# An instance norm on one core: 28 of 32 units joined in pairs, with rows of 64 KB

## The chip, the core and the metric

The kernel runs on one core of a Trainium2 chip. Its time is the device time of one execution in microseconds (us); the time before is the median of three runs. A profile, taken by the hardware profiler in one execution, shows what each engine did: TensorE (PE), VectorE (DVE), ScalarE (ACT), GpSimd (POOL) and SyncE (SP), and the 16 DMA engines that move data between the device memory and the on-chip memory, which has 128 partitions. Matmuls read on-chip memory and write a second, small one (PSUM).

## What is computed

```python
B, G, C_per_g, H, W = 4, 8, 16, 256, 256          # x: float32, 134 MB
mu = x.mean(axis=(3, 4), keepdims=True)
var = ((x - mu) ** 2).mean(axis=(3, 4), keepdims=True)
out = (x - mu) / np.sqrt(var + 1e-5) * gamma[None, :, :, None, None]
```

There are 512 channels (4 x 8 x 16) of 65,536 numbers. Each is brought to mean 0 and variance 1 and multiplied by its own gamma; there are 128 gammas, used again for each of the four images.

## The kernel before

The 512 channels are worked on in 32 units of 16 channels. A channel lies in 8 partitions (`S = 8`), so that a unit is one tile of 128 partitions x 8192 numbers: 4 MB, in rows of 32 KB, one contiguous stretch of `x`. Six tiles (`slots`, `AHEAD = 6`, 24 MB together) take the units in turn: unit u lies in slot u % 6. There is no automatic ordering; each engine runs its instructions in the order in which the loop writes them, and waits by semaphore for the data that it needs.

Ahead of the loop, POOL writes a small block of zeros to the first unit of the output (`touch`, lines 52 to 54) and loads the gammas as one row (`g_row`). Then the first six loads are issued, four on SP's queue, two (units 1 and 3) on ACT's. POOL builds `navg`, a 128 x 128 matrix that holds -1/65536 where two partitions belong to the same channel. Eight matrix products (line 86; the profile counts two passes of each) spread the gammas over the partitions: `g_col` has one column for each of the eight groups of 16 channels.

Then, for each unit:

1. VectorE sums every row (line 105), while ScalarE squares every number and sums the squares (line 106; the squares themselves go to `junk` and are not used).
2. TensorE multiplies `navg` with the two columns of sums (line 114). This gives each partition minus the mean and minus the mean square of its channel, in `ps`.
3. VectorE forms minus the variance (line 115), ScalarE the root (line 119), VectorE the reciprocal (line 123) and the product with gamma (line 125).
4. VectorE scales the tile in place, (x - mean) x scale (line 128).
5. ScalarE's queue issues the store of the tile (line 132).
6. SP's queue issues the load of unit u + 6 into the same slot (line 134, by the helper at line 48). It waits until the store of unit u has landed.

So all steady loads are on SP's queue (q1 in the profile), all stores on ACT's (q10); the DMA engines serve both.

Of the kernel before, what the change touches and what calls it, by code (L numbers as in the profile page):

```python
# [1 line left out]

# [4 lines left out]

F32 = mybir.dt.float32
U8 = mybir.dt.uint8
ALU = mybir.AluOpType  # L10
ACTF = mybir.ActivationFunctionType
AX = mybir.AxisListType


@with_exitstack
def kernel(
    ctx: ExitStack,
    tc: tile.TileContext,
    x: bass.AP,
    gamma: bass.AP,  # L20
    out: bass.AP,
):
    nc = tc.nc
    B, G, C, H, W = x.shape
    P = nc.NUM_PARTITIONS
    HW = H * W
    n_ch = B * G * C
    S = 8
    K = P // S
    F = HW // S  # L30
    U = n_ch // K
    NG = (G * C) // K
    AHEAD = 6
    assert HW % S == 0 and (G * C) % K == 0

    xv = x.rearrange("b g c h w -> (b g c h w)").rearrange("(u p f) -> u p f", p=P, f=F)
    ov = out.rearrange("b g c h w -> (b g c h w)").rearrange("(u p f) -> u p f", p=P, f=F)
    gv = gamma.rearrange("g c -> (g c)")

    data = ctx.enter_context(tc.tile_pool(name="data", bufs=1))  # L40
    singles = ctx.enter_context(tc.tile_pool(name="singles", bufs=1))
    psum = ctx.enter_context(tc.tile_pool(name="psum", bufs=4, space=bass.MemoryType.PSUM))
    ctx.enter_context(tc.manual_schedule())

    slots = [data.tile([P, F], F32, name=f"xt{i}") for i in range(AHEAD)]

    def load(u, queue):
        queue.dma_start(out=slots[u % AHEAD][:], in_=xv[u])  # L48


    g_row = singles.tile([1, G * C], F32, name="g_row")
    touch = singles.tile([16, 128], F32, name="touch")
    nc.vector.memset(touch[:], 0.0)  # L53
    nc.gpsimd.dma_start(out=ov[0][0::S, 0:128], in_=touch[:])  # L54
    nc.gpsimd.dma_start(out=g_row[:], in_=gv[None, :])  # L55
    for u in range(AHEAD):
        load(u, nc.scalar if u in (1, 3) else nc.sync)


    eps_t = singles.tile([P, 1], F32, name="eps_t")  # L60
    nc.gpsimd.memset(eps_t[:], 1e-5)
    one = singles.tile([1, 1], F32, name="one")
    nc.gpsimd.memset(one[:], 1.0)
    navg = singles.tile([P, K, S], F32, name="navg")
    nc.gpsimd.memset(navg[:], -1.0 / HW)  # L65
    nc.gpsimd.affine_select(  # L66
        out=navg[:], in_=navg[:], pattern=[[-S, K], [0, S]], compare_op=ALU.is_ge,
        fill=0.0, base=0, channel_multiplier=1,
    )
    nc.gpsimd.affine_select(  # L70
        out=navg[:], in_=navg[:], pattern=[[S, K], [0, S]], compare_op=ALU.is_ge,
        fill=0.0, base=S - 1, channel_multiplier=-1,
    )
    navg_w = navg[:].rearrange("p k s -> p (k s)")
    root_eps = singles.tile([P, 1], F32, name="root_eps")
    nc.scalar.activation(out=root_eps[:], in_=eps_t[:], func=ACTF.Sqrt)  # L76
    g_rep = singles.tile([1, NG, K, S], F32, name="g_rep")
    g_ps = psum.tile([P, NG], F32, name="g_ps", bufs=1)
    g_col = singles.tile([P, NG], F32, name="g_col")

    nc.vector.tensor_copy(  # L81
        out=g_rep[:],
        in_=g_row[:].rearrange("o (n k) -> o n k", n=NG).unsqueeze(3).to_broadcast([1, NG, K, S]),
    )
    for n in range(NG):
        nc.tensor.matmul(  # L86
            out=g_ps[:, n : n + 1],
            lhsT=g_rep[:, n].rearrange("o k s -> o (k s)"),
            rhs=one[:],
            start=True, stop=True,  # L90
        )
    nc.vector.tensor_copy(out=g_col[:], in_=g_ps[:])  # L92

    junk = singles.tile([P, F], U8, name="junk")

    st = singles.tile([P, U, 2], F32, name="st")
    nvar = singles.tile([P, U], F32, name="nvar")
    std = singles.tile([P, U], F32, name="std")
    rstd = singles.tile([P, U], F32, name="rstd")
    scale = singles.tile([P, U], F32, name="scale")  # L100

    squares = []
    for u in range(U):
        t = slots[u % AHEAD]
        nc.vector.reduce_sum(out=st[:, u, 0:1], in_=t[:], axis=AX.X)  # L105
        square = nc.scalar.activation(  # L106
            out=junk[:], in_=t[:], func=ACTF.Square, accum_out=st[:, u, 1:2],
        )
        if u:

            tc.declare_no_dep(square.ins, squares[-1].ins, reason="junk, ordered by the root between")
        squares.append(square)
        ps = psum.tile([P, 2], F32, name="ps")
        nc.tensor.matmul(out=ps[:], lhsT=navg_w, rhs=st[:, u], start=True, stop=True)  # L114
        nc.vector.tensor_scalar(  # L115
            out=nvar[:, u : u + 1], in0=ps[:, 0:1], scalar1=ps[:, 0:1],
            scalar2=ps[:, 1:2], op0=ALU.mult, op1=ALU.add,
        )
        nc.scalar.activation(  # L119
            out=std[:, u : u + 1], in_=nvar[:, u : u + 1], func=ACTF.Sqrt,  # L120
            bias=eps_t[:], scale=-1.0,
        )
        nc.vector.reciprocal(out=rstd[:, u : u + 1], in_=std[:, u : u + 1])  # L123
        g = u % NG
        nc.vector.tensor_mul(  # L125
            out=scale[:, u : u + 1], in0=rstd[:, u : u + 1], in1=g_col[:, g : g + 1],
        )
        nc.vector.tensor_scalar(  # L128
            out=t[:], in0=t[:], scalar1=ps[:, 0:1], scalar2=scale[:, u : u + 1],
            op0=ALU.add, op1=ALU.mult,  # L130
        )
        nc.scalar.dma_start(out=ov[u], in_=t[:])
        if u + AHEAD < U:
            load(u + AHEAD, nc.sync)


# [1 line left out]
_INS = ['x', 'gamma']  # L138
_OUTS = [((4, 8, 16, 256, 256), 'float32')]


# [23 lines left out]
```

## Time and profile before

| | |
|---|---|
| Time, median of 3 runs | 627.45 us (626.88 to 627.5) |
| Profiled execution: span from the first to the last instruction | 625.4 us |
| Moved | 268.46 MB, mean 429 GB/s over the span |
| VectorE busy | 443.4 us (71%) |
| ScalarE busy | 238.8 us (38%) |
| TensorE, GpSimd busy | 21.4 us, 2.4 us |
| Loads, stores | 32 each, of 4 MB |
| SP's queue waiting for a store to land | 534.9 us, 26 times |

The profile gives no time of its own for the profiled execution beside the span; the median of the runs is 2.05 us above it.

How to read it: the span is cut in 40 equal slices, and a digit is the busy share of a slice in tenths (9 is 90% or more); for DMA it is the mean of the 16 engines, with the GB/s beneath. A group's line names source line, engine, operation, what it writes <- what it reads, the shapes and the count; then busy us and mean ns of one; then the idle time of the engine ahead of these instructions and what ended it. A line on DMA issues ends with the KB of one and the median time from issue to landing. A line of waits gives the us in total, the times and the longest. In the chain of waits, each piece has a start, a length and a name; "another core or an unknown queue" stands where no releaser could be named. A line of windows gives the stretch, the busy time (and number of instructions) of PE, weight loads, DVE, ACT and POOL, the granted clock of TensorE, the DMA share and the GB/s. The trace also holds a record of each DMA packet: its start, queue, size and duration.

### The profile page before, as it was taken

The numbers are of one execution on the slowest core, as the hardware profiler recorded it, in microseconds if no ns is written. First come the engines' busy times: TensorE is split into PE (matmuls) and PEld (weight loads), VectorE is DVE, ScalarE is ACT, GpSimd is POOL, SyncE is SP. The second block draws the span as 40 slices with busy tenths as digits, with TensorE's granted clock in tenths as the row PEclk, the third lists the DMA queues.
The fourth block names the chain that finished last, engine by engine and source line by source line (L and its number), as shares of the span: only waits on it lengthen the run. The fifth ranks groups of instructions, "written<-read, shape, count | busy, mean of one in ns | idle before, by whom it ended". The sixth has DMA issues, their size and how long they took to land.

```text
span 625.4 us, 631 instructions
## 1 busy us (share of the span) xinstructions
PE 21.4 (3%) x80; PEld 19.5 (3%) x80; DVE 443.4 (71%) x163; ACT 238.8 (38%) x98; POOL 2.4 (0%) x11
## 2 busy tenths in 40 slices
PE   0200000000000000000000000000000000000000
PEld 0200000000000000000000000000000000000000
DVE  0588999999776687666776767867668676686730
ACT  0444444444443244432344423444224442244400
POOL 1000000000000000000000000000000000000000
DMA  8999999999999999999999999999999999999998
GB/s 369 436 402 436 436 436 436 436 434 424 434 436 432 432 428 434 436 436 436 436 434 423 434 436 432 436 428 434 434 436 436 436 436 432 425 434 434 434 432 363
DMA packets 9282, 268.46 MB, mean 429 GB/s; under 512 B 1072, under 2 KB 1088, under 8 KB 1088
## 3 DMA queue, kind: packets, MB, share of 16 engines
q10 hardware_dynamic: 4896, 142.61, 52.9%
q1 hardware_dynamic: 4320, 125.83, 46.7%
q0 software_dynamic: 64, 0.01, 0.0%
q14 instruction: 2, 0.02, 0.0%
HBM read 134.22 MB, written 134.23 MB: 429 GB/s over the span
## 4 chain that ended last, share of the span: by engine, by line
another core or an unknown queue 61%; DMA 17%; DVE 15%; SPq 1%; PE 1%; issue 0%; ACT 0%
DVE st L105 10%; DMA xt<-in_x_dram 10%; DMA out_dram<-xt 8%; DVE xt L128 5%; SPq L48 1%; PE ps L114 1%; ACT std L119 0%; DVE nvar L115 0%; DVE rstd L123 0%; DVE scale L125 0%
## 5 line engine op out<-in xcount | busy, mean ns | idle before, releaser
L105 DVE TENSOR_REDUCE st<-xt 128x1 f32<-128x8192 f32 x32 | 277.9, 8685 | 100.8 <-DMA xt<-in_x_dram 100.8
L106 ACT ACTIVATE junk<-xt 128x8192 uint8<-128x8192 f32 x32 | 225.0, 7030 | 275.6 <-DMA xt<-in_x_dram 232.4
L128 DVE TENSOR_SCALAR xt<-xt,ps,scale 128x8192 f32<-128x8192 f32 x32 | 145.6, 4551 | 1.2
L119 ACT ACTIVATE std<-nvar,eps_t 128x1 f32<-128x1 f32 x32 | 9.4, 295 | 79.6 <-DVE nvar L115 79.6
L114 PE MATMUL ps<-st,navg 128*128 128x2 f32 x64 | 17.8, 348 | 557.6 <-DVE st L105 557.6
L114 PEld LDWEIGHTS ps<-st,navg 128*128 128x128 f32 x64 | 16.0, 311 | 559.4 <-issue 559.4
L115 DVE TENSOR_SCALAR nvar<-ps 128x1 f32<-128x1 f32 x32 | 9.2, 288 | 23.8 <-PE ps L114 23.8
L123 DVE RECIPROCAL rstd<-std 128x1 f32<-128x1 f32 x32 | 5.3, 164 | 11.6 <-ACT std L119 11.6
L81 DVE COPY g_rep<-g_row 1x1024 f32<-1x1024 f32 x1 | 0.7, 681 | 14.2 <-DMA g_row<-in_gamma_dram 14.2
L106 ACT ACTIVATION_READ_ACCUMULATOR junk<-xt 128x1 f32 x32 | 6.0, 187 | 0.0
L125 DVE TENSOR_TENSOR scale<-rstd,g_col 128x1 f32<-128x1 f32 x32 | 5.1, 160 | 1.1
L86 PE MATMUL g_ps<-one,g_rep 1*128 1x1 f32 x16 | 3.5, 347 | 16.1 <-DVE g_rep L81 16.1
L86 PEld LDWEIGHTS g_ps<-one,g_rep 1*128 1x128 f32 x16 | 3.5, 326 | 16.1 <-issue 16.1
L92 DVE COPY g_col<-g_ps 128x8 f32<-128x8 f32 x1 | 0.2, 167 | 3.7 <-PE g_ps L86 3.7
L76 ACT ACT_TABLE_LOAD x1 | 1.3, 1283 | 1.7 <-PEq L149 1.7
L53 DVE MEMSET touch<- 16x128 f32 x1 | 0.2, 165 | 0.9 <-PEq L149 0.9
L54 POOL DMA_DIRECT2D out_dram<-touch x1 | 0.6, 617 | 0.8 <-DVE touch L53 0.8
L55 POOL DMA_DIRECT2D g_row<-in_gamma_dram x1 | 0.5, 484 | 0.0
L66 POOL TENSOR_SCALAR_AFFINE_SELECT navg<-navg 128x128 f32<-128x128 f32 x1 | 0.4, 398 | 0.1
L70 POOL TENSOR_SCALAR_AFFINE_SELECT navg<-navg 128x128 f32<-128x128 f32 x1 | 0.4, 397 | 0.1
L65 POOL MEMSET navg<- 128x128 f32 x1 | 0.2, 231 | 0.0
L76 ACT ACTIVATE root_eps<-eps_t 128x1 f32<-128x1 f32 x1 | 0.2, 203 | 0.0
(6 smaller groups left out, 0.6 us busy)
## 6 DMA issues: line engine op xcount, KB each, us to landing
out_dram<-xt ACTq DMA_DIRECT2D x32, 4096.0 KB, 62.5
xt<-in_x_dram SPq DMA_DIRECT2D x30, 4096.0 KB, 38.5
xt<-in_x_dram ACTq DMA_DIRECT2D x2, 4096.0 KB, 31.7
out_dram<-touch POOLq DMA_DIRECT2D x1, 8.0 KB, 9.1
g_row<-in_gamma_dram POOLq DMA_DIRECT2D x1, 0.5 KB, 13.3
```

The costliest lines, as they stand in the source:

```text
L48: queue.dma_start(out=slots[u % AHEAD][:], in_=xv[u])
L76: nc.scalar.activation(out=root_eps[:], in_=eps_t[:], func=ACTF.Sqrt)
L81: nc.vector.tensor_copy(out=g_rep[:], in_=g_row[:].rearrange("o (n k) -> o n k", n=NG).unsqueeze(3).to_broadcast([1, NG, K, S]),)
L86: nc.tensor.matmul(out=g_ps[:, n : n + 1], lhsT=g_rep[:, n].rearrange("o k s -> o (k s)"), rhs=one[:], start=True, stop=True,)
L105: nc.vector.reduce_sum(out=st[:, u, 0:1], in_=t[:], axis=AX.X)
L106: square = nc.scalar.activation(out=junk[:], in_=t[:], func=ACTF.Square, accum_out=st[:, u, 1:2],)
L114: nc.tensor.matmul(out=ps[:], lhsT=navg_w, rhs=st[:, u], start=True, stop=True)
L115: nc.vector.tensor_scalar(out=nvar[:, u : u + 1], in0=ps[:, 0:1], scalar1=ps[:, 0:1], scalar2=ps[:, 1:2], op0=ALU.mult, op1=ALU.add,)
L119: nc.scalar.activation(out=std[:, u : u + 1], in_=nvar[:, u : u + 1], func=ACTF.Sqrt, bias=eps_t[:], scale=-1.0,)
L123: nc.vector.reciprocal(out=rstd[:, u : u + 1], in_=std[:, u : u + 1])
L125: nc.vector.tensor_mul(out=scale[:, u : u + 1], in0=rstd[:, u : u + 1], in1=g_col[:, g : g + 1],)
L128: nc.vector.tensor_scalar(out=t[:], in0=t[:], scalar1=ps[:, 0:1], scalar2=scale[:, u : u + 1], op0=ALU.add, op1=ALU.mult,)
```

## The change

The units 0 and 1 and the last two stay as they are (16 channels, 4 MB, 8 partitions for each channel). The 28 between are joined in pairs to 14 units of 32 channels: 8 MB, four partitions for each channel, 16,384 numbers (64 KB) in each partition, again one contiguous stretch. So there are 18 units: 2 small, 14 large, 2 small. The six slots become three of 8 MB (`pairs`), of which a small unit takes a half. `follower` says which unit's store a load has to follow: the last owner of any half that it overwrites. The loads of units 0 to 3 are issued at the start; the load of unit 4 follows the store of unit 1, that of unit 5 the store of unit 2, and so on; those of units 16 and 17 both follow the store of unit 13.

In a large unit VectorE sums and scales 16,384 numbers in a partition with one instruction each, and ScalarE squares the two halves with two instructions, into two columns of sums; a second matrix product adds the second half's sum of squares. All loads are on SP's queue. `touch` is gone. Gammas and averaging matrix are there once for each size of unit (8 rows of 16 gammas, and 4 rows of 32), and one matrix product with an identity for each spreads the gammas.

The diff, cut to its core:

```diff
-    S = 8
-    K = P // S
-    F = HW // S
-    U = n_ch // K
-    NG = (G * C) // K
-    AHEAD = 6
+    GC = G * C
+    F = HW // 8
+    HALVES = 6
+    SIZES = [1, 1] + [2] * 14 + [1, 1]
+    SPAN = {1: 8, 2: 4}
+    CH = {1: P // 8, 2: P // 4}
...
-    slots = [data.tile([P, F], F32, name=f"xt{i}") for i in range(AHEAD)]
+    pairs = [data.tile([P, 2 * F], F32, name=f"xt{i}") for i in range(HALVES // 2)]
+    units = []
+    at = 0
+    for n in SIZES:
+        pair, half = (at % HALVES) // 2, at % 2
+        first = at * CH[1]
+        flat = slice(first * HW, (first + CH[n]) * HW)
+        units.append((
+            n, first % GC, pairs[pair][:, half * F : (half + n) * F],
+            xf[flat].rearrange("(p f) -> p f", p=P), of[flat].rearrange("(p f) -> p f", p=P),
+        ))
+        at += n
+    U = len(units)
+    follower = {}
+    owner = {}
+    at = 0
+    for u, n in enumerate(SIZES):
+        for h in range(at, at + n):
+            if h % HALVES in owner:
+                follower[u] = max(follower.get(u, -1), owner[h % HALVES])
+            owner[h % HALVES] = u
+        at += n
...
-    nc.vector.memset(touch[:], 0.0)
-    nc.gpsimd.dma_start(out=ov[0][0::S, 0:128], in_=touch[:])
-    nc.gpsimd.dma_start(out=g_row[:], in_=gv[None, :])
-    for u in range(AHEAD):
-        load(u, nc.scalar if u in (1, 3) else nc.sync)
+    for n in (1, 2):
+        nc.gpsimd.dma_start(out=g_rows[n][:], in_=gv.rearrange("(n k) -> n k", k=CH[n]))
+    for u in range(U):
+        if u not in follower:
+            load(u, nc.sync)
...
+    # ident, 8 x 8: a memset and two affine_selects on gpsimd
+    # navg_w[n] for n in (1, 2): a memset and two affine_selects each, as before for one
...
+    for n in (1, 2):
+        rows, K, S = GC // CH[n], CH[n], SPAN[n]
+        nc.vector.tensor_copy(
+            out=g_rep[:], in_=g_rows[n][:].unsqueeze(2).to_broadcast([rows, K, S]),
+        )
         nc.tensor.matmul(
-            out=g_ps[:, n : n + 1],
-            lhsT=g_rep[:, n].rearrange("o k s -> o (k s)"),
-            rhs=one[:],
-            start=True, stop=True,
-        )
-    nc.vector.tensor_copy(out=g_col[:], in_=g_ps[:])
+            out=g_ps[:], lhsT=g_rep[:].rearrange("n k s -> n (k s)"),
+            rhs=ident[0:rows, 0:rows], start=True, stop=True,
+        )
+        nc.vector.tensor_copy(out=g_col[n][:], in_=g_ps[:])
...
-    for u in range(U):
-        t = slots[u % AHEAD]
-        nc.vector.reduce_sum(out=st[:, u, 0:1], in_=t[:], axis=AX.X)
-        square = nc.scalar.activation(
-            out=junk[:], in_=t[:], func=ACTF.Square, accum_out=st[:, u, 1:2],
-        )
+    for u, (n, first, t, _, dst) in enumerate(units):
+        nc.vector.reduce_sum(out=st[:, u, 0:1], in_=t, axis=AX.X)
+        for h in range(n):
+            square = nc.scalar.activation(
+                out=junk[:], in_=t[:, h * F : (h + 1) * F], func=ACTF.Square,
+                accum_out=st[:, u, 1 + h : 2 + h],
+            )
...
-        nc.tensor.matmul(out=ps[:], lhsT=navg_w, rhs=st[:, u], start=True, stop=True)
+        nc.tensor.matmul(
+            out=ps[:], lhsT=navg_w[n], rhs=st[:, u, 0:2], start=True, stop=n == 1,
+        )
+        if n == 2:
+            nc.tensor.matmul(
+                out=ps[:, 1:2], lhsT=navg_w[n], rhs=st[:, u, 2:3], start=False, stop=True,
+            )
...
-        nc.scalar.dma_start(out=ov[u], in_=t[:])
-        if u + AHEAD < U:
-            load(u + AHEAD, nc.sync)
+        nc.scalar.dma_start(out=dst, in_=t)
+        for v in range(U):
+            if follower.get(v) == u:
+                load(v, nc.sync)
```

## The prediction

> **What bounds the kernel now.** I read the page first, then the chain, the waits of SP's queue, the windows of the drain and the timeline of the last unit, and last the trace's packet records (start, queue, size, duration of each DMA packet). From the page:
>
> ```profile
> span 625.4 us, 631 instructions
> DMA  8999999999999999999999999999999999999998
> GB/s 369 436 402 436 436 436 436 436 434 424 434 436 432 432 428 434 436 436 436 436 434 423 434 436 432 436 428 434 434 436 436 436 436 432 425 434 434 434 432 363
> L105 DVE TENSOR_REDUCE st<-xt 128x1 f32<-128x8192 f32 x32 | 277.9, 8685 | 100.8 <-DMA xt<-in_x_dram 100.8
> L128 DVE TENSOR_SCALAR xt<-xt,ps,scale 128x8192 f32<-128x8192 f32 x32 | 145.6, 4551 | 1.2
> xt<-in_x_dram SPq DMA_DIRECT2D x30, 4096.0 KB, 38.5
> out_dram<-xt ACTq DMA_DIRECT2D x32, 4096.0 KB, 62.5
> ```
>
> The DMA engines are busy in every slice; VectorE is idle 100.8 us for loads. The chain goes through SP's issues in a fixed beat:
>
> ```profile
> 179.46 0.33 SPq L48
> 179.79 18.95 another core or an unknown queue
> 198.77 0.03 issue
> 198.80 0.33 SPq L48
> ```
>
> One 4 MB load and one 4 MB store per 19.35 us. SP's own waits say for what:
>
> ```profile
> SPq L48 <- DMA out_dram<-xt: 534.9, 26, 59.7
> ```
>
> A load goes when the store of its slot's last owner lands. The drain, by windows (last columns: DMA share, GB/s) and timeline:
>
> ```profile
> 590.00:600.00 10.00, 0.56 (x2) 0.50 (x2) 8.83 (x5) 3.16 (x3) 0.00 (x0) 1.00 0.98 423
> 610.00:615.00 5.00, 0.00 (x0) 0.00 (x0) 0.00 (x0) 0.00 (x0) 0.00 (x0) 1.00 1.00 433
> 585.74 8.69 DVE L105 TENSOR_REDUCE st<-xt 128x1 f32<-128x8192 f32 x1 [4.33 <-DMA xt<-in_x_dram]
> 596.21 4.55 DVE L128 TENSOR_SCALAR xt<-xt,ps,scale 128x8192 f32<-128x8192 f32 x1
> 600.80 0.34 ACTq L132 DMA_DIRECT2D out_dram<-xt  x1
> ```
>
> The last store is issued at 600.80 and its first packets start only at 613.3: older stores keep the engines full, so the fill and the drain hide all computing. The packet records: on one engine rows of 32 KB start 1209.4 ns apart and the 4-byte completion packet takes 6 ns; each engine has 512 rows, 512 x 1.2094 = 619.2 us. With the first row at 1.8, some 0.55 us extra on it, 1.1 us extra around the first store (39.9 to 43 us), and 1.3 us from the end of data (624.1) to the end of the span, that is the whole span. The profile gives no other time for its execution than the span; the median of the runs, 627.45, is 2.05 above it, and I carry these 2.05 over.
>
> **Rows and completions (removed).** 28 units of 8 rows per engine in each direction become 14 with rows of 64 KB: 224 pairs of rows join per engine, and 28 of 64 completions go. The line through 4 bytes (6 ns) and 32 KB (1209.4) gives 65536 x 36.73 ps + 5.9 = 2413 ns for a 64 KB row, 5.9 less than two. 224 x 5.9 = 1.32 us, and 28 x 6 ns = 0.17: **-1.5 us**. Bounds: 0 beside the 0.17 if all cost goes by bytes; -2.0 by the packet durations (512 bytes 27 ns, 32 KB 1213: 8.2 fixed). I take the spacing, since it makes up the span.
>
> **Computing of a joined unit (C).** Reduce 17.2 (twice 8.685 less a fixed 0.15; at most 17.4). Between reduce and scaling the last unit shows 1.78, and a second matmul adds about 0.55 (a pair of passes takes 0.57 in the chain). Scaling 8.8 (twice 4.55 less 0.28, which a one-column operation takes; at most 9.1). C = 28.35, bound 28.9; the two squares, 2 x 7.2 on ScalarE, lie beside the reduce. A small unit stays at 15.0. VectorE needs 28.35 per 38.6 us beat: hidden, and the slot's slack (three slots x 38.6 less C less two shared transfers of 38.6) is 10 us where it was 62 (6 x 19.35 - 15.0 - 2 x 19.35).
>
> **Setup: touch out, gammas, identity and second averaging matrix in, all loads on SP.** GpSimd gains about 2 us (0.23 + 0.40 + 0.40 for a matrix, 0.5 for a DMA issue), done by about 5 us and needed after 20. Gamma landed at 15.3; 16 matmuls become 2. In VectorE's queue the two copies of each gamma stand ahead of the first reduce; even at 18 they are covered, because the engines owe L0 to L3, S0 and S1 until 81 us (1.8 + 0.55 + 1.1 + 8 x 9.68), and S2 is ready by about 78: S0 begins at 32 at a start of 16, L2 has by then had 10.3 of its 19.3 us, needs 13.5 more with two rows of bytes for one of S0's (the turns are shown below), lands at 48, and 28.35 + 1.1 follow. If that cover went, the price is at most 2 us: L4 starts when S1 has landed. SP issues four loads back to back in 2 us and then waits for stores only; nothing else is queued there. On ScalarE squares of the next unit wait behind the store's issue as before (8 waits, 5.4 us at most). For 28 us loads run from one queue: the drain runs full from one queue (433), so I take 0; at worst the windows' 419 for 28 us, +0.9. Without the touch the first stores may pay what the first loads did, 0 to +0.7; I take 0, as they pay with it.
>
> **The drain (a new wait).** Write L and S for load and store of the new units 0 to 17. The records show that a DMA engine with both queues waiting takes one row from each in turn (q1 at 4.787, q10 at 5.997). If it still does so, a 64 KB store row gets two thirds against a 32 KB load row. That decides the end, where L16 and L17 are small and S14 and S15 large. Let 0 be the end of L15 on the engines, one row after S13. L16 is there by then (landing 0.9 after the mean engine, issue to first packet 1.0, against a row of 2.4). S14 owes 8 rows: 8 turns of 2.41 + 1.21 = 29.0, and L16 is done too. S15 is ready at 0.9 + 28.35 + 1.1 = 30.35. Alone, L17 gets two rows, to 31.4; its other six cost 6 x 3.62, to 53.1. It lands at 54.0, C is 15.0, issue 1.1: S17 starts at 70.1 and is done at 79.8. The engines owe S14, L16, L17, S15, S16, S17 = 77.3 in all. So they stand empty 2.5, of which some 0.5 returns because the engines, 1.1 apart, restart in step: 2.0. Were S15 ready before the second row of L17 begins at 30.2, L17 would end 2.4 later: 4.4. The border lies within the spread of the engines, and the worst served one sets the landing: I take **+3.6 us**.
>
> Here a rule of the Trainium skill differs from the row: DMA: Bandwidth & Descriptors, section "Queues, rings and completion order", lets an engine drain a whole packet, typically 9 to 17 descriptors, before it switches queues. By it L16 and L17 would pass in two blocks, land at about 40, and the drain would stay full: 626.0. The records show switching after each row, and they decide. The same page, "Latency and other measured facts", warns of per-partition row pitches at large powers of two: full rate at 512 KiB, loss from 2 MiB. The change doubles the pitch; no run here shows the effect.
>
> **Sum.** 627.45 - 1.5 + 3.6 = 629.55, say 629.6 (span 627.5).
>
> **Rivals.**
> - *The drain stays covered.* If store landing to next load takes over 2.4 us (expected 2.0), L15 ends two rows after S13: S14 has one row less to give, L17 gets three rows alone, ends at 48.5, S17 at 75.2 against 74.9 owed. No gap: 627.45 - 1.5 = 626.0. For it: the engines are 1.1 us apart, so the margin of 0.4 is thin. Against: the landing waits for the slowest engine, for which the delay is shortest. This is the case on the other side.
> - *Turns go by bytes, or the rows are split into 32 KB again.* By bytes L2 shares half with S0 and lands at 52 to 55, S2 is ready at 81.5 to 84, the engines run dry at 81 and L4 starts at 83: a gap of 0.5 to 2.0 in the fill, none in the drain: up to 628.0. Split: L17 ends early, only 0.17 is saved, 627.3.
> - *64 KB rows stream worse.* If the joined part runs as the windows' 424 of 80 to 100 us and not 433, 2% of 540 us is 11: about 637. For it: nothing in the steady part (1213 ns for nearly each row). With a covered drain it makes the kernel slower by over 0.2% from 12 ns more per large row (224 x 12 = 2.7 against -1.5).
>
> **How the numbers follow.** A measurement of this kernel can tell about 0.2% (1.25 us) from no change. Chances: drain gap 0.55, covered drain 0.24, turns by bytes or split rows 0.09, worse rows 0.12. The gap's own range is 627.9 (smaller gap) to 631.8 (4.4, 0.7 for cold stores, 0.7 less saved in rows). Of its 0.55, 0.38 is over 628.7. Faster is the covered drain, 0.24; slower 0.38 + 0.12 = 0.50; the same 0.17 + 0.09 = 0.26. The range reaches from a covered drain with the larger saving, 625.6, to 631.8; worse rows are left out.
>
> **What would show it.** Right: DMA of 9 in all slices but the first and the last two; a beat of 38.61 to 38.65 us per joined unit (38.71 before); large packets of 65536 bytes spaced 2.413 us; VectorE's last reduce starting after 598 us, and the last store's packets starting at once, with engines empty for 2 to 4.5 us ahead of them. Wrong: last store queued behind S16 (covered drain); a dip of GB/s near 81 us (turns by bytes); rows above 2.42 us or 32 KB packets throughout; a gap at every beat, which would mean that the 10 us of slack were not there.

## The result, and the profile after

The changed kernel takes 632.66 us (median of five runs, 631.61 to 633.22) against 627.45: a ratio of 1.0084, 95% interval 1.0071 to 1.0096. That is 5.2 us slower; the forecast was 2.15 us slower, and the time lies above its range. The profiled execution took 632.26 us for a span of 630.6, so 1.66 us lie around the span (the prediction carried over the 2.05 by which the median of before lies above its span). Further below, a run that took over 1.5% longer than the fastest of its kernel is left out of the ratios, but not out of the medians.

From the page of the changed kernel (lines are those of the changed file: the loads are L74, the stores L174):

```profile
span 630.6 us, 471 instructions
DMA  8999999999999999999999999999999999999986
GB/s 366 432 399 449 420 461 412 453 424 441 457 407 445 420 449 412 458 407 457 407 458 407 457 407 457 407 457 407 457 416 449 424 441 437 428 405 432 464 368 272
DMA packets 5250, 268.46 MB, mean 426 GB/s; under 512 B 640, under 2 KB 640, under 8 KB 640
L139 DVE TENSOR_REDUCE st<-xt 128x1 f32<-128x16384 f32 (+1 forms) x18 | 275.8, 15322 | 148.3 <-DMA xt<-in_x_dram 148.3
L170 DVE TENSOR_SCALAR xt<-xt,ps,scale 128x16384 f32<-128x16384 f32 (+1 forms) x18 | 141.6, 7869 | 0.7
xt<-in_x_dram SPq DMA_DIRECT2D x14, 43.9
out_dram<-xt ACTq DMA_DIRECT2D x14, 44.5
```

Computing costs no more than it did (the two VectorE groups sum to 417.4 us, before 423.5). The rate alternates between 407 and 457, as 6.5 rows of 2.414 us to a slice of 15.8 us would make it, if a row counts in the slice in which it starts; the mean of the two is 432, close to the 434 of before. The loss is at the right end: 368 and 272 in the last two slices, and the busy digits 8 and 6. SP waits for the same thing as before, the store of the slot's last owner (its issues from L5 at 118.28 us to L16 at 548.28 us lie 39.1 us apart on the mean; the prediction expected 38.61 to 38.65):

```profile
SPq L74 <- DMA out_dram<-xt: 539.9, 13, 79.3
```

The end of the chain of waits of the changed kernel (start, duration, engine, tile, line):

```profile
553.00 17.23 DVE st L139
...
572.43 8.82 DVE xt L170
581.25 8.61 DVE st L139
...
591.63 4.55 DVE xt L170
596.18 4.23 another core or an unknown queue
600.43 8.70 DVE st L139
...
610.91 4.55 DVE xt L170
```

Before, the last reduce started at 585.74 and the last store, issued at 600.80, then queued until 613.3. Now the last reduce starts at 600.43, 4.23 us of waiting ahead of it, the last store is issued at 615.49, and 15 of the 16 engines have nothing queued ahead of it. The timeline of the same stretch shows why the last reduces start so late:

```profile
553.00 17.22 DVE L139 TENSOR_REDUCE st<-xt 128x1 f32<-128x16384 f32 x1 [10.31 <-DMA xt<-in_x_dram]
581.28 0.34 ACTq L174 DMA_DIRECT2D out_dram<-xt  x1
596.21 0.34 ACTq L174 DMA_DIRECT2D out_dram<-xt  x1
600.43 8.69 DVE L139 TENSOR_REDUCE st<-xt 128x1 f32<-128x8192 f32 x1 [4.25 <-DMA xt<-in_x_dram]
615.49 0.34 ACTq L174 DMA_DIRECT2D out_dram<-xt  x1
```

Both reduces waited for loads (in brackets: idle time ahead, and what ended it). The windows of the drain (columns as before: DMA share and GB/s last):

```profile
600.00:613.00 13.00, 0.56 (x2) 0.50 (x2) 11.39 (x5) 7.42 (x3) 0.00 (x0) 1.00 0.94 406
613.60:616.20 2.60, 0.00 (x0) 0.00 (x0) 1.86 (x1) 0.00 (x0) 0.00 (x0) 1.00 0.12 50
617.00:626.00 9.00, 0.00 (x0) 0.00 (x0) 0.00 (x0) 0.00 (x0) 0.00 (x0) 1.00 0.95 408
626.30:629.00 2.70, 0.00 (x0) 0.00 (x0) 0.00 (x0) 0.00 (x0) 0.00 (x0) 1.00 0.06 24
```

Two holes. From 613.6 to 616.2 the engines wait for S17: that is the hole that the prediction describes. From 626.3 to 629.0 the share is 0.06, one engine of 16: 15 have finished, and one still works off its rows of S17. This second hole was not in the prediction.

The packet records single that engine out. They hold no engine number; I followed the 16 engines by joining each packet to the one whose end meets its start. Sums over all engines don't depend on this joining, figures of one engine do, by up to some 1.7 us where rows of several engines start together. A row is called slow by what it takes over the usual duration of its size (1213 ns for 32 KB, 2418 ns for 64 KB). Two executions of the changed kernel are shown, the second from the first experiment:

```
per engine, us                     before         changed        changed, again
slow rows after 62 us, median      0.17           0.8            2.85
  the same, worst engine           0.53           6.59           5.38
slow rows in all, worst engine     2.23           8.61           7.29
empty after 600 us, most engines   0.01           2.5 to 3.1     2.7 to 5.4
  the engine that ended last       0.01           0.01           0.01
last load lands, first/last engine 584.3/585.4    584.4/600.0    587.6/603.1
engines end, median/last           623.5/624.1    626.15/629.06  629.2/629.7
```

A load counts as landed only with its slowest engine. Before, the engines finish a load within 1.1 us of each other all the way. In the changed kernel this spread is 0.45 us for unit 0, 2.7 for unit 4, 0.5 for unit 6, 4 for unit 10, 7 for units 12 to 15, and 15.6 for the last load; in the second execution it is about 4 for units 9 to 15, and 15.5 for the last load. The engine that ended last was never idle: -1.2 us by larger rows and fewer completions (224 x 4.8 ns by the measured spacings, and 0.17), +6.4 by slow rows (8.61 less 2.23), -0.4 by less idle time, together +4.8, against 4.96 measured (629.06 less 624.10).

### The profile page after: what moved, and what is told of

Same layout as the page of the kernel before. It is cut to its first block, busy times and chain, and to the rows that moved or that the text cites. A ratio compares the mean times of both kernels' runs of the same rounds, so it can differ in the third digit from the quotient of the medians.

```text
span 630.6 us, 471 instructions
## 1 busy us (share of the span) xinstructions
PE 17.2 (3%) x68; PEld 16.0 (3%) x68; DVE 429.0 (68%) x94; ACT 234.7 (37%) x84; POOL 4.0 (1%) x16
## 4 chain that ended last, share of the span: by engine, by line
DMA 63%; DVE 26%; another core or an unknown queue 7%; PE 1%; issue 0%; ACT 0%; SPq 0%
DMA xt<-in_x_dram 35%; DMA out_dram<-xt 28%; DVE st L139 16%; DVE xt L170 8%; PE ps L150 1%; PE ps L154 0%; ACT std L161 0%; DVE nvar L157 0%; SPq L74 0%; DVE rstd L165 0%; DVE scale L167 0%
## 5 line engine op out<-in xcount | busy, mean ns | idle before, releaser
L139 DVE TENSOR_REDUCE st<-xt 128x1 f32<-128x16384 f32 (+1 forms) x18 | 275.8, 15322 | 148.3 <-DMA xt<-in_x_dram 148.3
L170 DVE TENSOR_SCALAR xt<-xt,ps,scale 128x16384 f32<-128x16384 f32 (+1 forms) x18 | 141.6, 7869 | 0.7
L161 ACT ACTIVATE std<-nvar,eps_t 128x1 f32<-128x1 f32 x18 | 5.3, 295 | 71.6 <-DVE nvar L157 71.6
L150 PE MATMUL ps<-st,navg 128*128 128x2 f32 x36 | 10.0, 349 | 582.3 <-DVE st L139 582.3
L157 DVE TENSOR_SCALAR nvar<-ps 128x1 f32<-128x1 f32 x18 | 5.2, 287 | 19.4 <-PE ps L154 16.4
L154 PE MATMUL ps<-st,navg 128*128 128x1 f32 x28 | 7.9, 352 | 0.0
L165 DVE RECIPROCAL rstd<-std 128x1 f32<-128x1 f32 x18 | 3.0, 164 | 6.5 <-ACT std L161 6.5
L167 DVE TENSOR_TENSOR scale<-rstd,g_col 128x1 f32<-128x1 f32 x18 | 2.9, 159 | 0.6
L123 PEld LDWEIGHTS g_ps<-ident,g_rep 8*128 8x128 f32 (+1 forms) x4 | 1.0, 308 | 10.5 <-issue 8.6
```

Of the source, the lines that this page charges most:

```text
L123: nc.tensor.matmul(out=g_ps[:], lhsT=g_rep[:].rearrange("n k s -> n (k s)"), rhs=ident[0:rows, 0:rows], start=True, stop=True,)
L139: nc.vector.reduce_sum(out=st[:, u, 0:1], in_=t, axis=AX.X)
L150: nc.tensor.matmul(out=ps[:], lhsT=navg_w[n], rhs=st[:, u, 0:2], start=True, stop=n == 1,)
L154: nc.tensor.matmul(out=ps[:, 1:2], lhsT=navg_w[n], rhs=st[:, u, 2:3], start=False, stop=True,)
L157: nc.vector.tensor_scalar(out=nvar[:, u : u + 1], in0=ps[:, 0:1], scalar1=ps[:, 0:1], scalar2=ps[:, 1:2], op0=ALU.mult, op1=ALU.add,)
L161: nc.scalar.activation(out=std[:, u : u + 1], in_=nvar[:, u : u + 1], func=ACTF.Sqrt, bias=eps_t[:], scale=-1.0,)
```

## The experiments

Four groups of kernels, each run beside the kernel before on the same chip (another chip for each group); ratios are to that kernel, with 95% intervals.

**The changed kernel again.** Nothing is edited.

> The changed kernel once more, for the spread between executions. Seen so far in its trace: one DMA engine lost 6.2 us after 50 us to load rows that took longer than 2418 ns, the other 15 lost 0.1 to 2.5 us; that engine ended 2.9 us after the others and its late landings left the others empty for 2.8 us near 614 us. If this belongs to the change, a single late engine with 4 to 8 us of stretched load rows is seen again and the time is 631 to 634 us. If it was chance in one execution, the trace shows no engine over 2 us and the time scatters down to 627.

Measured: 632.94 us, ratio 1.0079 (1.0059 to 1.0099). The loss repeats. Of the four runs, one took 641.63 us, the others 631.12 to 632.99. Its hole ahead of S17 is longer:

```profile
614.50:619.00 4.50, 0.00 (x0) 0.00 (x0) 4.00 (x1) 0.00 (x0) 0.00 (x0) 1.00 0.20 87
```

In this execution all engines but one end together, and the hole itself is the larger part of the loss (eight engines stood empty 4.4 to 5.4 us); in the first it was the late engine. Both go with a last load that lands unevenly: 15.6 and 15.5 us lie between its first and its last engine.

**The same kernel with rows of 32 KB.** The joined units stay; each transfer is cut into rows of 32 KB.

```diff
-        queue.dma_start(out=t, in_=src)
+        queue.dma_start(out=t, in_=src, max_dma_last_dim=32768)
-        nc.scalar.dma_start(out=dst, in_=t)
+        nc.scalar.dma_start(out=dst, in_=t, max_dma_last_dim=32768)
```

> The changed kernel with every load and store cut into 32 KB descriptors: same 8 MB transfers, same three slots, same waits. Theory A (the 64 KB load row is what gets stretched): no engine loses more than 1 us after 50 us, both queues share equally so that no drain gap opens, 0.17 us of completions saved: 627.3 us (626.5 to 628.2). Theory B (three slots: the load queue runs empty between loads and the first rows of a load are stretched, whatever their size): one late engine remains, 631 to 633 us.

Measured: 627.81 us, ratio 1.0011 (1.0001 to 1.0020). Its page, and the window that was a hole:

```profile
span 625.8 us, 471 instructions
DMA  8999999999999999999999999999999999999997
DMA packets 8835, 268.46 MB, mean 429 GB/s; under 512 B 641, under 2 KB 641, under 8 KB 641
```

```profile
613.00:617.00 4.00, 0.00 (x0) 0.00 (x0) 0.00 (x0) 0.00 (x0) 0.00 (x0) 1.00 1.14 492
```

Slow rows after 62 us are down to 0.09 us per engine, the spread to 1.6 us from unit 8 on (2.8 at most), and both holes are gone (a share over 1 means no more than full). Three slots, joined units, computing of 28.3 us per unit and the new setup are all still there: nearly the whole loss goes with the rows (5.1 of the 5.6 us between the two kernels on this chip). The hole in the drain goes too, as the prediction had it for rows of 32 KB.

**Rows of 32 KB in the loads alone.** Only the first of the two edits.

> The changed kernel with 32 KB descriptors for loads alone; stores keep 64 KB rows. Theory A: load rows are not stretched; half of the row saving stays (0.65 + 0.17 us), but a load gets one third of an engine against a store in progress, so the drain may stand empty for 2 to 4 us: 627 to 631 us. Theory B: a late engine as in the changed kernel, 631 to 634 us.

Measured: 657.25 us, ratio 1.0454 (1.0400 to 1.0508), which is 28 us. No theory expected this. In the drain the engines stand half empty for 15 us:

```profile
602.00:617.00 15.00, 0.99 (x4) 0.93 (x4) 13.40 (x6) 1.58 (x2) 0.00 (x0) 1.00 0.53 225
```

In the records an engine still takes one row from each queue in turn, so 32 KB load rows get a third of it against 64 KB store rows. Slow rows after 62 us come to 17 us per engine on the mean (6.9 in loads, 10.5 in stores), and the rate dips in the steady part too (333 and 365 GB/s in the two slices around 362 us). That loads fall behind stores all the way is what these turns would make of it; it was not followed unit by unit.

**Rows of 32 KB in the stores alone.** Only the second edit.

> The changed kernel with 32 KB descriptors for stores alone; loads keep 64 KB rows, so a load gets two thirds of an engine against a store and the last loads share equally. Half of the row saving stays (0.65 + 0.17 us). If stretching belongs to 64 KB load rows, some rows over 2418 ns remain but the drain stays covered: 627 to 630 us. If unequal turns alone break the overlap of slots, as the opposite mixture did (657 us), it is over 640 us with engines empty in the steady part.

Measured: 633.26 us, ratio 1.0098 (1.0083 to 1.0113). No hole in the drain, as 64 KB load rows have the upper hand there; but 4.9 us of slow rows per engine after 62 us, 4.5 of them in the loads, on all engines alike (3.1 to 6.9). The loss of the changed kernel is reached without its hole, and with the engines close together: the spread is 1.0 to 3.0 us from unit 5 on. So slow rows cost time without a drift as wide as in the changed kernel.

**Rows of 32 KB in the two stores of the drain.** This takes away what the prediction's term of 3.6 us rests on, and leaves the rest.

```diff
-        nc.scalar.dma_start(out=dst, in_=t)
+        nc.scalar.dma_start(out=dst, in_=t, max_dma_last_dim=32768 if u in (14, 15) else 65536)
```

> The changed kernel with the stores of units 14 and 15 alone cut into 32 KB descriptors, so that the last two small loads share an engine equally with them; all else keeps 64 KB rows. Theory A1 (the loss is the drain: a late engine needs 3.6 us for each row of the last load against a 64 KB store row, the last load lands late and all engines stand empty for 3 to 5 us): the empty stretch near 614 us shrinks below 1.5 us and the time falls to 627.5 to 630 us. Theory A2 (the loss is the stretched 64 KB load rows of one engine itself, 6 us, and the empty stretch only hides behind it): no change, 631 to 634 us.

Measured: 631.17 us (ten runs, 628.0 to 633.95), ratio 1.0053 (1.0039 to 1.0067). The hole is closed; its windows read:

```profile
600.00:613.00 13.00, 0.56 (x2) 0.50 (x2) 11.82 (x5) 5.94 (x3) 0.00 (x0) 1.00 0.99 426
613.00:617.00 4.00, 0.00 (x0) 0.00 (x0) 0.02 (x1) 0.00 (x0) 0.00 (x0) 1.00 1.04 451
```

The engines lose 0.1 us there in the records. By the ratios about 1.6 us come back (1.0079 to 1.0053; the intervals just overlap). The other 3.3 us stay: in the profile, which is of the longest of the ten runs, 4.6 us of slow rows per engine after 62 us, some 8 to 9 on the worst; one engine ended 3.9 us after the median. Most of these rows lie between 200 and 440 us, ahead of the two stores that were changed.

**Rows of 16 KB in the joined units.** The opposite direction, for the fixed price of a row: 448 rows more per engine than with 32 KB throughout.

```diff
-        queue.dma_start(out=t, in_=src)
+        queue.dma_start(out=t, in_=src, max_dma_last_dim=16384 if units[u][0] == 2 else 32768)
-        nc.scalar.dma_start(out=dst, in_=t)
+        nc.scalar.dma_start(out=dst, in_=t, max_dma_last_dim=16384 if n == 2 else 32768)
```

> The changed kernel with the large units' loads and stores cut into 16 KB descriptors (the small ones stay at 32 KB). It has 448 rows per engine more than with 32 KB throughout, which took 627.8 us. If every row has a fixed cost of 5.9 ns, as the line through 4 bytes and 32 KB says, the time is 627.8 + 2.6 = 430.4 + 200 = 630.4 us, with rows spaced 607.7 ns. If the cost goes by bytes alone, it stays at 627.8 us, with rows spaced 604.7 ns. Nothing is stretched in either case.

Measured: 630.45 us, ratio 1.0054 (1.0040 to 1.0067), 2.64 us over the kernel with 32 KB (on another chip; 2.7 by the ratios). Row spacing is 607.0 ns; 448 x (2 x 607.0 - 1209.4) gives 2.1, and at the 5.9 ns of the prediction it would be 2.6. The time alone can't give the price, since 1.1 us of slow store rows per engine, in one stretch between 100 and 150 us, come in addition. By the spacing a row has a fixed price of 4.6 ns (2 x 607.0 - 1209.4); from 32 to 64 KB it is 4.8 (2 x 1209.4 - 2414.0). So the rows of 64 KB do save 224 x 4.8 = 1.1 us; it is just outweighed.

**Rows of 64 KB for units 4 to 10 alone.** The first and last joined units go in 32 KB, so that the fill and the drain are those of the good kernel (`max_dma_last_dim=65536 if 4 <= u <= 10 else 32768` on both lines).

> The changed kernel with 64 KB rows for units 4 to 10 alone (loads and stores); the rest, the fill and the drain among it, in 32 KB rows. If 64 KB rows are stretched in mixed traffic wherever they stand, some 1 to 3 us of stretched rows are seen between 90 and 390 us and none after, and the time is 628 to 631 us. If the loss sits in the drain alone, nothing is lost and half of the row saving comes through: 627.2 us.

Measured: 635.79 us, ratio 1.0155 (1.0131 to 1.0180), worse than 64 KB in all joined units. The rate over the span, and the window of its dip:

```profile
span 633.2 us, 471 instructions
GB/s 369 426 424 433 431 464 402 439 422 439 455 414 443 447 414 460 402 455 402 460 402 460 422 433 449 402 428 431 431 431 424 435 435 437 364 414 439 410 433 282
545.00:550.00 5.00, 0.00 (x0) 0.00 (x0) 2.12 (x1) 0.00 (x0) 0.00 (x0) 1.00 0.63 269
```

The 64 KB part is where 402 and 460 alternate. The dip to 364 comes 150 us after it: from the seam on, where rows of both sizes meet, the spread goes from 2.7 us (unit 10) to 8.9 (unit 11) and 11 (unit 13), and from 545 us on most engines stand empty 2.4 to 2.9 us. By unit 16 the spread is back at 4.1, and 7.2 for the last load. Neither expectation held: of 3.5 us of slow rows per engine, 1.1 lie between 90 and 390 us and 2.4 after, nearly all of these in rows of 32 KB. That the seam pulled the engines apart is argued from its place in time alone.

**Each joined transfer as two of 64 partitions.**

```diff
-        queue.dma_start(out=t, in_=src)
+        for p in ((0, P),) if units[u][0] == 1 else ((0, 64), (64, P)):
+            queue.dma_start(out=t[p[0] : p[1]], in_=src[p[0] : p[1]])
```

and the same for the stores.

> The changed kernel with each 8 MB transfer issued as two of 64 partitions (64 KB rows, 4 MB each), so that half of a slot can be loaded when half of its store has landed. If the three coarse slots cause the spread of the engines, it is gone and the row saving stays: 626 to 628 us. If 64 KB rows cause it: as the changed kernel, 630 to 634 us. If a transfer into 64 partitions does not reach all engines equally, it is far slower: over 700 us.

Measured: 881.61 us (849.49 to 890.25).

```profile
span 880.6 us, 539 instructions
DMA packets 5699, 268.46 MB, mean 305 GB/s; under 512 B 1089, under 2 KB 1089, under 8 KB 1089
```

After 62 us the median 64 KB load row takes 3971 ns instead of 2418, the median store row 2645, while the DMA engines are busy (9 tenths or more in 38 of 40 slices). It says nothing on the question asked, as another cost, which stays open, covers it. The Trainium skill (DMA: Bandwidth & Descriptors, section "Rules for kernel authors") holds splitting by partition halves to be useless, since both halves use the same engines. Here it was harmful: the four runs lie 217 to 257 us above the 632.94 us of the changed kernel, which ran on another chip.

**The kernel before with the new setup.** No touch, all six first loads on SP; units and rows as before.

```diff
-    touch = singles.tile([16, 128], F32, name="touch")
-    nc.vector.memset(touch[:], 0.0)
-    nc.gpsimd.dma_start(out=ov[0][0::S, 0:128], in_=touch[:])
-        load(u, nc.scalar if u in (1, 3) else nc.sync)
+        load(u, nc.sync)
```

> The kernel before with two parts of the change's setup alone: no block of zeros written to the output at the start, and all six first loads on SP's queue. The prediction took 0 for both, with 0 to +0.7 us for the first stores and up to +0.9 us for loads from one queue: 627.3 us if 0, up to 628.9 us if both are paid.

Measured: 627.46 us, ratio 1.0010 (1.0001 to 1.0019) against 626.84 in the same group: +0.6 us. That is the ratio of the all-32 KB kernel, 1.0011, from another chip: with 32 KB rows, joining 28 units costs nothing that this measurement finds beyond the setup. Both intervals begin at 1.0001, so that the 0.6 itself is barely clear of noise.

**The kernel before with four slots.** `AHEAD = 4`: less slack, 32 KB rows throughout.

> The kernel before with four 4 MB slots in place of six, nothing else: 32 KB rows, but the load queue holds one load or less ahead, as in the changed kernel. Theory A: rows stay at 1213 ns; at most some 1 to 2 us for an empty stretch near 48 us, where the first stores have landed late: 627.5 to 629.5 us. Theory B: stretched first rows of loads and a late engine: 631 to 634 us.

Measured: 632.96 us, ratio 1.0092 (1.0074 to 1.0110). The time is that of the changed kernel, but the way is another: two hard stops, 1.5 us near 52 us and 2.5 us near 617 us, and 1.1 us of slow rows, all of them before 120 us.

```profile
50.00:53.50 3.50, 0.00 (x0) 0.00 (x0) 3.50 (x2) 0.49 (x1) 0.00 (x0) 1.00 0.60 215
616.50:619.30 2.80, 0.00 (x0) 0.00 (x0) 1.80 (x1) 0.00 (x0) 0.00 (x0) 1.00 0.44 187
```

So little slack costs time at the fill and the drain, and not by itself a slow row in between (from 120 us on they come to about 0.1 us per engine).

**The kernel before with three slots.** `AHEAD = 3`.

> The kernel before with three slots of 4 MB: 32 KB rows, and a load is issued only when the load ahead of it is done or nearly so, so that its first row mostly meets an empty load queue. It is slower for lack of slots (over 640 us); what counts is the first rows of loads. If a load that starts on an empty queue beside running stores is stretched whatever its row size, its first 32 KB rows are over 1213 ns by 50 ns or more on average, as the first 64 KB rows of the changed kernel were over 2418 by 15 to 176. If it takes 64 KB rows, they stay within 20 ns of 1213.

Measured: 662.96 us in one run, without an interval.

```profile
span 660.9 us, 633 instructions
GB/s 381 381 254 409 416 414 418 426 444 422 399 433 430 407 418 421 438 391 436 442 418 377 444 428 397 411 444 426 381 432 440 416 407 418 440 411 442 414 264 254
```

The rate dips all along. Load rows of 32 KB are slow by 12.7 us per engine after 62 us here, store rows by 0.1. Slow rows are thus no property of 64 KB rows alone. From 100 us on they come in bursts of 0.7 to 1.5 us per engine, on the nine loads whose first row starts 1.0 to 2.2 us after the issue, as the load ahead ends; the loads whose first row starts 3.5 us or more after the issue have 0.1 us or less.

## Why the prediction was right or wrong

**Rows and completions: the spacing right, the term wrong.** This is the step that failed. A 64 KB row is spaced 2414.0 ns on an undisturbed engine (2413 forecast), and the 16 KB kernel confirms a fixed price per row, of 4.6 to 4.8 ns and not 5.9, so that 1.2 us and not 1.5 were there to gain. But the step took this spacing as the whole cost of a 64 KB row, with bounds of 0 to -2.0 us that left out any loss. The engine that decides the profiled run paid 6.4 us more in slow rows than the worst one before, where the term had only the 1.5 us gained. On one chip 64 KB rows cost 632.94 - 627.81 = 5.1 us net, the hole in the drain included; without that hole it is about 3.5 us (see the sum), where the step had a gain of 1.5. The rival "64 KB rows stream worse" had the cause, at a chance of 0.12, but as 2% on every row, worth 11 us. What happened is uneven: 0.8 us on the median engine and 6.6 on one of 16 after 62 us in the first profile, 2.85 and 5.4 in the second. A load lands with its slowest engine, so that the slowest counts most. The prediction itself named rows above 2.42 us as a sign that it was wrong, and they are what the records show.

**Computing of a joined unit: right.** Reduce 17.23, the step between 2.21, scaling 8.83: 28.27 us against 28.35.

**The fill: right.** S2 was issued at 77.67 (about 78 forecast), ahead of the 81 us at which the engines would have run dry.

```profile
77.67 0.34 ACTq L174 DMA_DIRECT2D out_dram<-xt  x1
```

**Setup: taken as 0, was 0.6** (0.1 to 1.2 by the interval), within the bounds given. In slow rows until 62 us the engines lose 1.77 us with the new setup on the kernel before, 1.50 with the old; so the records show 0.3 of the 0.6. The changed kernel loses 2.04, with 32 KB rows 1.54.

**The drain: mechanism right, size by luck.** The records show rows of L16 and S14 in turn, one for one (starts at 553.1, 554.3, 556.7, 557.9), as the prediction took from the records of before. The Trainium skill (DMA: Bandwidth & Descriptors, section "Queues, rings and completion order") has an engine drain typically 9 to 17 descriptors before it switches; these records don't show that. The hole ahead of S17 is there, 2.9 us on 13 engines (2.0 to 4.4 forecast) and up to 5.4 in the second profile, and S17's rows start at once. But the working has most engines sharing L17 with S15. On the median engine L17 ran alone, from 574.8 to 584.5: S15 was issued only at 581.28, since L15 landed at 553.0, after 545.7 on the median engine. On the late engine L17 did share with S15, until 600.0, and that set the landing. A spread of 1.1 us was assumed; for L15 and L17 it was 7.3 and 15.6. And closing the hole brought only about 1.6 of the 5 us back, where the term was 3.6.

**The sum.** Forecast: -1.5 + 0 + 3.6 = +2.1. Measured: +5.2. By the group of experiments: setup +0.6, row size +5.1 net, everything else -0.1 (627.81 less 627.30, less the 0.6); together 5.6, which is what lay between the two kernels on that chip. The hole in the drain is part of the 5.1 and not to be added to it. In the prediction's own terms, and with the 1.6 us that closing the hole brought back: rows about +3.5 where it had -1.5, drain about +1.6 where it had +3.6, setup +0.6 where it had 0. These parts come from different chips and are good to about 1 us. So the right direction, slower, came with the wrong parts: the term for the drain was too large and hid a part of what the rows cost.

**The account of the span before.** It is said to be whole, but 1.8 + 0.55 + 1.1 + 619.2 + 1.3 is 624.0, 1.4 short of 625.4. The rest lies in the completions (64 x 6 ns = 0.4), in 0.5 us of slow rows on the engine that ended last, and in some 0.5 us that was not placed. The forecast carries the measured time over and doesn't rest on this sum.

**The pitch.** The prediction cited a rule on row pitch and could not test it. (The Trainium skill, DMA: Bandwidth & Descriptors, section "Latency and other measured facts", has 207 GB/s at 512 KiB and calls 214 full, so "full rate" is rounded.) With 32 KB rows the joined units have the doubled pitch, and their rows are spaced 1209 ns as before: no cost at this pitch.

**What stays open** is what makes a row slow. That the row size decides it in this kernel is shown: the same kernel in 32 KB rows has next to none. How it does so is not. Of the slow time in 64 KB load rows after 62 us, some 1.5 of 2.0 us per engine lie in the first row of a transfer in the drain experiment, and 1.3 of 2.4 in the changed kernel's second profile; with 32 KB stores alone it is 1.6 of 3.6, so it is not only that. The three slots suggest that it depends on when a load starts and what the engines do then (they show slow rows of 32 KB; with four slots and 32 KB rows there are next to none after 120 us), but no run separates row size from that timing.

## What to carry to other kernels

A row twice as long saves a few nanoseconds of fixed cost, here 1.1 us in 627, but its spacing on an undisturbed engine is not its whole cost: here slow rows and engines that drifted apart took 5 us more than they took with short rows. A transfer lands with its slowest engine, so follow the packets by engine, and not only the mean rate, before taking the saving. Be careful with rows of unequal size: against the kernel before, 32 KB loads beside 64 KB stores cost 28 us and a change of size in mid-run 9, where 32 KB throughout cost 0.5 and 64 KB in all joined units 5.6. It depends on the mixture: 32 KB in the stores alone cost 6, in the last two large stores alone 4. Joining units for fewer instructions can be had apart from longer rows, and with three large slots in place of six it then cost next to nothing.

## What the hardware showed that was not expected

- Unequal rows share unequally: with 32 KB load rows against 64 KB store rows in all joined units, 657.25 us, and slow rows of 17 us per engine.
- Sixteen engines that finish each load within 1.1 us of each other in the kernel before are 7 us apart from unit 12 on with 64 KB rows in one execution and about 4 us in another, and 15.6 and 15.5 us at the last load.
- A load issued to an empty load queue while stores run starts its first row some 4 us later (in the changed kernel L4, issued at 82.1, first row at 86.0; with 32 KB rows issued at 121.2, first row at 125.5), where 1.0 us had been assumed.
- Transfers over 64 partitions ran at a mean of 305 GB/s, their load rows at 3971 ns instead of 2418 in the median.
